# A decoder step on one core: reciprocal roots on ScalarE, the first factors on another queue, a longer warm-up, and a new order of squares, pooling steps and low parts

## The chip, the core and the metric

The kernel runs on one NeuronCore of a Trainium2 chip. TensorE multiplies matrices into PSUM, VectorE, ScalarE and GpSimd work on rows of 128 partitions, and SyncE (SP) issues most DMAs. The metric is device time in microseconds (us) of one execution.

## The reference

One step of a decoder layer over 288 rows: 256 new positions of one sequence and 8 x 4 new positions of running sequences.

```
h = rmsnorm(x, norm1_g)
a, gate, z = split(h @ w_in + b_in)                 # 2048 -> 3 x 1024
u = a * sigmoid(gate)
c = silu(layernorm(depthwise_conv31(history + u)))  # 1024 channels
d = window_sum(z) / count - z                       # windows 2, 4, 8, 16
p = (d @ pool_w per group) * pool_scale
x = x + concat(c, p) @ w_out                        # 2048 -> 2048
f = square(relu(rmsnorm(x, norm2_g) @ w_ff1))       # 2048 -> 8192
y = rmsnorm(x + f @ w_ff2, norm_f)
```

It also returns the last 30 rows of u and the last 15 of z. Everything is float32.

## The kernel before

Channels lie on the partitions, the 288 rows along the free dimension. Each float32 operand is split into a high part, the value rounded to TensorE's fp32r format, and a low part, the rest. A product of 128 x 128 weights with 128 x 288 values is then three matmuls: high by high, low by high, high by low. That makes 8112 matmuls of 288 columns, and TensorE's order of them is the kernel's spine.

*Weights.* `load` brings a block of 1024 x 256 in two DMAs of 512 KB into a ring of six raw tiles, and `split_part` makes both parts of each, into a ring of five pairs. ScalarE always casts the high part (L274). The low part comes in one of three ways, by a letter in the table `WAYS` (L73): V, VectorE subtracts (L279); G, GpSimd subtracts in two halves (L282); D, ScalarE writes the negated high part (L276) and GpSimd issues a DMA that adds the raw weights from memory to it (L277). A key such as `c3` names a stage, with one letter for each of its four parts; the fallback is the key's first letter. The feed-forward stage, `ff`, is all V.

*Stages.* Input projection in the order `c0 c1 c2 c3 c4 p3 c5 p2 P3 c6 p1 P2 p0 P1 c7 P0`: a `c` is a pair of 128 conv channels and their gates, a `p` one pooling group of 256 channels, a `P` that group's small product with pool_w. Each `c` and `p` has 96 matmuls, each `P` 12. Then w_out over the pooling half (eight groups of 48 matmuls), w_out over the conv half, and four chunks of w_ff1 and w_ff2.

*The first stage.* c0 and c1 run together, over eight pairs of 128 input rows. For each pair `first_split` loads x and weights, casts the high weights (L364, L371), scales x by the norm's gain into `hx` (L367 on VectorE for the first, L369 on ScalarE), and forms the low parts (L373, L376). Nine float32 products of a constant run ahead, as a warm-up (L214). `squares` sums x squared for the first norm (ScalarE L418, VectorE L420 to L422), held back by a small copy that reads the third pair's high weights (L413); `rsqrt_sums` turns the sums into reciprocal roots (Sqrt on ScalarE, then reciprocal and a correction step on VectorE, L249 to L256), and `spread` copies them to all partitions by a product with the identity matrix. The row that results multiplies the projections later (L445, L483).

*Convolution.* VectorE does 30 of the 31 taps of each channel block (L461) at low priority: the block stands in `later()`, which adds to the scheduler's priority number. A smaller number goes first.

*Order.* A scheduler with a planned timeline lays each engine's instructions out ahead of the run, by priority among those that are ready in its plan. `tc.issue_after(x)` puts an instruction behind x on its engine. In the middle of the kernel `mm` chains every matmul behind the last one (up to the product P1); `between` hands a function to `gemm` that puts a norm's small products ahead of a given k of a group.

*The end.* The last product's rows are summed, `inverse_root` (L231 to L236) forms the factors, and `finish` (L715 to L721) scales and stores in pieces, in turn on SP's and ScalarE's DMA queues.

Of the kernel before, what the change touches and what calls it, by code (L numbers as in the profile page):

```python
# [72 lines left out]
WAYS = {"c2": "GVGV", "c3": "GDGG", "c4": "GDGD", "p3": "GDDG", "c5": "GDGD", "c": "GGGV", "p": "GVVG", "w0": "VV", "w": "GG", "ff": "VV"}  # L73
# [13 lines left out]
def trunk_kernel(ctx: ExitStack, tc: tile.TileContext, io):  # L87
# [110 lines left out]
    nc.sync.dma_start(vec[:, 0:NG], io["vec"][:, 0:NG])  # L198
# [8 lines left out]
    def load_table(func, src):  # L207

        return nc.scalar.activation(few[: src.shape[0], :], src, func)

    load_table(AF.Sqrt, ones[:, 0:1])
    warm = ms("warm")
    for j in range(9):
        nc.tensor.matmul(warm[:, 0, 0:P], ones, ones, start=True, stop=True)  # L214
# [16 lines left out]
    def inverse_root(mean, root, y, out):  # L231

        nc.vector.reciprocal(y, root)
        nc.vector.scalar_tensor_tensor(out=root, in0=mean, scalar=EPS, in1=y, op0=ALU.add, op1=ALU.mult)
        nc.vector.scalar_tensor_tensor(out=root, in0=root, scalar=-0.5, in1=y, op0=ALU.mult, op1=ALU.mult)
        nc.vector.scalar_tensor_tensor(out=out, in0=root, scalar=1.5, in1=y, op0=ALU.add, op1=ALU.mult)  # L236

    def rsqrt_sums(parts, scale, after=None):

        pq = ms("pt")
        pt = pq[:, 0, :]
        for n, t in enumerate(parts):
            for j in range(3):
                last = mm(pt[:TB, j : j + 1], t[:, j * TB : (j + 1) * TB], ones[:, 0:1], start=n + j == 0, stop=n == len(parts) - 1 and j == 2)
        st = const.tile([TB, 12], F32, name=nm("st"))
        s = [st[:, 3 * j : 3 * j + 3] for j in range(4)]
        nc.vector.tensor_scalar(s[0], pt[:TB, 0:3], scale * DC, EPS, op0=ALU.mult, op1=ALU.add)  # L249
        nc.scalar.activation(s[1], s[0], AF.Sqrt)  # L250
        if after is not None:
            load_table(after, s[1][:, 0:1])
        nc.vector.reciprocal(s[2], s[1])
        nc.vector.tensor_tensor(s[3], s[2], s[2], op=ALU.mult)
        nc.vector.scalar_tensor_tensor(out=s[3], in0=s[3], scalar=-0.5, in1=s[0], op0=ALU.mult, op1=ALU.mult)
        nc.vector.scalar_tensor_tensor(out=s[2], in0=s[3], scalar=1.5, in1=s[2], op0=ALU.add, op1=ALU.mult)  # L256
        return s[2], pq[:, 1, :T], last
# [99 lines left out]
    hx, firsts = [], []  # L357

    def first_split(k0):
# [5 lines left out]
        for k in range(k0, k0 + 2):  # L365
            if k == 0:
                nc.vector.tensor_scalar(hx[k][0], xT[:, k, :], v("norm1_g", k), None, op0=ALU.mult)  # L367
            else:
                nc.scalar.activation(hx[k][0], xT[:, k, :], AF.Copy, scale=v("norm1_g", k))  # L369
        for b in blocks[1:]:  # L370
            nc.scalar.copy(hi[:, b], raw[:, b])  # L371
        for b in blocks:
            nc.vector.tensor_tensor(lo[:, b], raw[:, b], f32(hi[:, b]), op=ALU.subtract)  # L373
# [37 lines left out]
    def squares():  # L411

        nc.scalar.copy(scratch[:, :, :, 0:1], f32(firsts[2][0])[:, 1, 1, 0:10].rearrange("p (n k t) -> p n k t", n=5, t=1))  # L413
        for q in range(8):
            xq = xT[:, 2 * q : 2 * q + 2, :]
            a = q // 4
            dst = scratch[:, 2 + q % 3] if q % 4 else tot[a]
            nc.scalar.activation(dst, xq, AF.Square)  # L418
            if q % 4:
                nc.vector.tensor_tensor(tot[a], tot[a], dst, op=ALU.add)  # L420
# [19 lines left out]
    def conv_pair(i, banks):  # L440
        up = u_all[:, i, 0:UO]
        us = samples(u_all[:, i, UO:UL], US)
        ta, gate = [b[:, :T] for b in banks]
        for b in (gate, ta):
            nc.vector.tensor_tensor(b, b, rb, op=ALU.mult)  # L445
        tg = tmpp.tile([P, 2, T], F32, name=nm("tg"), tag="ag", bufs=2)[:, 0, :]
        nc.scalar.activation(tg, gate, AF.Sigmoid, bias=v("b_in", 8 + i))
        for out, a, b in ((up[:, CH:UO], ta[:, :SEQ], tg[:, :SEQ]), (us[:, :, CH:US], samples(ta[:, SEQ:T], NS), samples(tg[:, SEQ:T], NS))):
            nc.vector.scalar_tensor_tensor(out=out, in0=a, scalar=v("b_in", i), in1=b, op0=ALU.add, op1=ALU.mult)
# [27 lines left out]
    def pool_group(g):  # L477
# [17 lines left out]
        first_sums = s[:, :, PH : PH + w - 1]  # L495
        nc.gpsimd.tensor_tensor(first_sums, first_sums, rcnt[:, None, w - 2 : 2 * w - 3].to_broadcast([P, 2, w - 1]), op=ALU.mult)
        nc.vector.scalar_tensor_tensor(out=d[:, :, 0:SEQ], in0=s[:, :, PH:ZO], scalar=1.0 / w, in1=z[:, :, PH:ZO], op0=ALU.mult, op1=ALU.subtract)
        news = [x[:, :, ZO:ZL].rearrange("p m (b t) -> p m b t", t=ZS)[:, :, :, PH:] for x in (s, z)]
        nc.gpsimd.tensor_scalar(news[0], news[0], 1.0 / w, None, op0=ALU.mult)
        nc.gpsimd.tensor_tensor(d[:, :, SEQ:T].rearrange("p m (b t) -> p m b t", t=NS), news[0], news[1], op=ALU.subtract)  # L500
        dh, dl = act2("dx", tag="p", bufs=4)
        nc.scalar.copy(dh, d)
        nc.vector.tensor_tensor(dl, d, f32(dh), op=ALU.subtract)
# [20 lines left out]
    def first_sums():  # L524
        diag.append(rsqrt_sums(squares(), 1.0 / D, AF.Sigmoid))
        return diag[0][2]

    def first_rows():
        pr, last = spread(diag[0])
        nc.scalar.copy(rb, pr)  # L530
        return last
# [16 lines left out]
    load_table(AF.Sqrt, f32(mixp[1][0])[:, 0:1])  # L548
# [12 lines left out]
    def ln_sums():  # L561
        ssc = None
        for c in cs:
            nc.vector.tensor_tensor(c, c, norm["mean"][:, None, :].to_broadcast([P, 2, T]), op=ALU.subtract)
            q = tmpp.tile([P, 2, T], F32, name=nm("q2"), tag="ag" if ssc is None else "ag2", bufs=2)
            nc.scalar.activation(q, c, AF.Square)
            if ssc is None:
                ssc = q
            else:
                nc.vector.tensor_tensor(ssc, ssc, q, op=ALU.add)  # L570
        nc.vector.tensor_tensor(ssc[:, 0, :], ssc[:, 0, :], ssc[:, 1, :], op=ALU.add)
        norm["sums"] = rsqrt_sums([ssc[:, 0, :]], 1.0 / DC, AF.Silu)
        return norm["sums"][2]

    def ln_rows():
        norm["rows"], last = spread(norm["sums"])
        return last

    BETWEEN = {5: {4: ln_mean}, 6: {6: ln_sums}, 7: {2: ln_rows}}
# [10 lines left out]
    for j, c in enumerate(cs):  # L590
        n = tmpp.tile([P, 2, T], F32, name=nm("n"), tag="ag", bufs=2)
        nc.vector.tensor_tensor(n, c, norm["rows"][:, None, :].to_broadcast([P, 2, T]), op=ALU.mult)  # L592
        for m in range(2):
            i = 2 * j + m
            nc.scalar.activation(n[:, m, :], n[:, m, :], AF.Silu, bias=v("ln_b", i), scale=v("ln_g", i))  # L595
        mh, ml = act2("mx")
        nc.scalar.copy(mh, n)  # L597
# [40 lines left out]
    def second_rows():  # L638
# [9 lines left out]
        nc.scalar.activation(root, mean, AF.Sqrt, bias=eps)  # L648
        inverse_root(mean, root, r2, r2)
# [57 lines left out]
    root, first, s_f = [cst[:TB, 2 + 3 * j : 5 + 3 * j] for j in range(3)]  # L707
    nc.scalar.activation(root, sums_f, AF.Sqrt, bias=eps[:TB, :])
    inverse_root(sums_f, root, first, s_f)
# [13 lines left out]
    finish(nc.vector, rows_f, ((0, 1), (1, 1), (2, 2), (4, 2), (6, 3), (9, 3)))  # L723
# [60 lines left out]
```

## Time and profile before

| | |
|---|---|
| three runs, us | 1084.15, 1084.95, 1085.42; median 1084.95 |
| the profiled execution, us | 1084.57, its span 1082.8 |
| busy in the span, us | TensorE 1071.5, VectorE 635.4, ScalarE 479.0, GpSimd 173.6 |
| GB/s read and written, mean over the span | 175 |

In the profile a row of the view by time has the start, the length in us, the engine (PE is TensorE, PEld its weight loads, DVE VectorE, ACT ScalarE, POOL GpSimd; a q behind the name is the engine's instruction queue, which issues DMAs), the line of the kernel, the operation, what it writes and reads, and how many it merges. What stands in brackets is the engine's idle time before it and what ended it. A row of the view by stretches has the stretch, its length, then busy us and count for PE, PEld, DVE, ACT and POOL, the granted TensorE clock, the DMA engines' share and GB/s; instructions that only touch a stretch's edge are counted. A row of the view by groups has the line, engine, operation, shapes and count, then the total busy us and the mean ns of one, and behind the second bar the idle time before them. The chain of waits gives the start, the length and what the time was spent on. Tile names: `whi`, `wlo` the parts of the weights, `hx` the scaled x, `dx` a pooling operand, `mx` a conv operand, `ac` and `pp` accumulators.

### The profile page before, as it was taken

What the parts mean: (1) busy time and instruction counts of PE and PEld (TensorE: products, weight loads), DVE (VectorE), ACT (ScalarE), POOL (GpSimd) and SP (SyncE); (2) the same over time, 40 slices, a digit from 0 to 9 for tenths busy, and PEclk for the clock granted to TensorE, in tenths of its full rate; (3) what the DMA queues carried; (4) which work ended last, traced back from release to release, by engine and by line L of the source; (5) the groups of instructions that cost most, each with busy time, mean ns of one, the idle gap of its engine ahead of it and who ended that gap; (6) DMA issues with size and microseconds to landing.
All of it is one profiled execution on the core that took longest, in us unless ns stands there. A gap on an engine that the chain in (4) does not pass through costs nothing.

```text
span 1082.8 us, 19572 instructions
## 1 busy us (share of the span) xinstructions
PE 1071.5 (99%) x8198; PEld 1069.9 (99%) x8198; DVE 635.4 (59%) x818; ACT 479.0 (44%) x585; POOL 173.6 (16%) x180
## 2 busy tenths in 40 slices
PE   9999999999999999999999999999999999999996
PEld 9999999999999999999999999999999999999996
DVE  8899999678655544445544444545544445554553
ACT  8654445475544433334443333444433334444441
POOL 0878979512000000000000000000000000000001
PEclk9999999999999999999999999999999999999998
DMA  9896468545555555555555555555555555555522
GB/s 325 281 273 185 137 196 239 176 152 177 173 164 170 172 166 169 174 164 169 171 168 168 175 165 169 174 167 167 174 165 168 174 169 165 173 166 168 173 78 88
DMA packets 58296, 190.71 MB, mean 176 GB/s; under 512 B 6240, under 2 KB 11232, under 8 KB 58208
## 3 DMA queue, kind: packets, MB, share of 16 engines
q1 hardware_dynamic: 56336, 184.35, 53.9%
q0 software_dynamic: 1008, 3.67, 1.9%
q8 instruction: 64, 1.05, 0.4%
q10 hardware_dynamic: 864, 1.44, 0.4%
q14 instruction: 24, 0.20, 0.1%
HBM read 185.16 MB, written 4.28 MB: 175 GB/s over the span
## 4 chain that ended last, share of the span: by engine, by line
PE 77%; issue 20%; ACT 1%; DVE 0%; DMA 0%; POOL 0%; POOLq 0%
PE ac L305 77%; PE pp L305 1%; DMA wr<-in_w 0%; ACT whi L274 0%; POOL xT L720 0%; ACT n L595 0%; DVE wlo L279 0%; PE pt L305 0%; PE pmean L305 0%; POOLq L770 0%; DVE xT L695 0%; DVE n L592 0%; ACT whi L364 0%; ACT mx L597 0%; DVE hx L367 0%
## 5 line engine op out<-in xcount | busy, mean ns | idle before, releaser
L274 ACT CAST whi<-wr 128x1024 fp32r<-128x1024 f32 (+1 forms) x332 | 348.0, 1049 | 551.4 <-PE ac L305 533.5
L279 DVE TENSOR_TENSOR wlo<-wr,whi 128x1024 fp32r<-128x1024 f32 x288 | 353.1, 1226 | 348.5 <-ACT whi L274 348.5
L305 PE MATMUL ac<-ax,whi 128*128 128x288 f32 x2048 | 351.0, 292 | 0.0
L305 PE MATMUL ac<-fx,whi 128*128 128x288 f32 x2048 | 350.2, 292 | 0.0
L305 PEld LDWEIGHTS ac<-ax,whi 128*128 128x128 f32 x2048 | 296.0, 187 | 0.0
L305 PEld LDWEIGHTS ac<-fx,whi 128*128 128x128 f32 x2048 | 295.6, 187 | 0.0
L305 PE MATMUL ac<-ax,wlo 128*128 128x288 f32 x1024 | 217.4, 292 | 0.0
L305 PE MATMUL ac<-fx,wlo 128*128 128x288 f32 x1024 | 216.4, 292 | 0.0
L305 PEld LDWEIGHTS ac<-ax,wlo 128*128 128x128 f32 x1024 | 162.6, 187 | 0.0
L305 PEld LDWEIGHTS ac<-fx,wlo 128*128 128x128 f32 x1024 | 162.3, 187 | 0.0
L305 PE MATMUL ac<-hx,whi 128*128 128x288 f32 x768 | 131.8, 295 | 1.2 <-DVE hx L367 1.2
L720 POOL TENSOR_TENSOR xT<-xT,rf 128x288 f32<-128x288 f32 x4 | 3.1, 795 | 800.1 <-ACT rf L724 800.1
L305 PEld LDWEIGHTS ac<-hx,whi 128*128 128x128 f32 x768 | 112.1, 190 | 1.4 <-ACT hx L369 1.4
L282 POOL TENSOR_TENSOR wlo<-wr,whi 128x512 fp32r<-128x512 f32 x74 | 100.3, 1410 | 35.3 <-ACT whi L274 34.3
L461 DVE SCALAR_TENSOR_TENSOR pc<-u_all,vec,pc 128x256 f32<-128x256 f32 x232 | 99.5, 483 | 1.9 <-ACT pc L458 0.7
L305 PE MATMUL ac<-hx,wlo 128*128 128x288 f32 x384 | 80.1, 294 | 0.0
L305 PEld LDWEIGHTS ac<-hx,wlo 128*128 128x128 f32 x384 | 61.1, 190 | 0.0
L305 PE MATMUL ac<-dx,whi 128*128 128x288 f32 x256 | 46.0, 296 | 0.0
L305 PE MATMUL ac<-mx,whi 128*128 128x288 f32 x256 | 45.1, 294 | 0.1
L664 DVE SCALAR_TENSOR_TENSOR t<-ac,r 128x576 f32<-128x576 f32 x32 | 24.2, 758 | 25.1 <-PE ac L305 25.1
L305 PEld LDWEIGHTS ac<-dx,whi 128*128 128x128 f32 x256 | 38.0, 188 | 0.2
L305 PEld LDWEIGHTS ac<-mx,whi 128*128 128x128 f32 x256 | 37.5, 188 | 0.6 <-ACT mx L597 0.4
(133 smaller groups left out, 533.6 us busy)
## 6 DMA issues: line engine op xcount, KB each, us to landing
wr<-in_w SPq DMA_DIRECT2D x335, 512.0 KB, 3.8
wlo<-in_w POOLq DMA_DIRECT2D x7, 512.0 KB, 7.7
xT<-in_xT SPq DMA_DIRECT2D x8, 288.0 KB, 7.3
wr<-in_w SPq DMA_DIRECT2D x5, 256.0 KB, 3.6
out_u_out<-u_all SPq DMA_DIRECT2D x1, 1208.0 KB, 9.3
u_all<-in_hist_c SPq DMA_DIRECT2D x8, 136.0 KB, 6.2
out_z_out<-z_all SPq DMA_DIRECT2D x1, 668.0 KB, 9.9
z_all<-in_hist_p SPq DMA_DIRECT2D x4, 152.0 KB, 7.5
```

The lines of the kernel that those rows point to most:

```text
L274: nc.scalar.copy(hi, raw)
L279: nc.vector.tensor_tensor(lo, raw, f32(hi), op=ALU.subtract)
L282: nc.gpsimd.tensor_tensor(lo[:, j : j + 2, :], raw[:, j : j + 2, :], f32(hi[:, j : j + 2, :]), op=ALU.subtract)
L305: last = nc.tensor.matmul(*args, **kw)
L461: nc.vector.scalar_tensor_tensor(out=dst, in0=up[:, w : w + SEQ], scalar=cwv[:, w : w + 1], in1=pc, op0=ALU.mult, op1=ALU.add)
L664: nc.vector.scalar_tensor_tensor(out=t, in0=bk[:, :, :T], scalar=0.0, in1=both(rows2[0]), op0=ALU.max, op1=ALU.mult)
L720: eng.tensor_tensor(xk, xk, r[:, None, :].to_broadcast([P, n, T]), op=ALU.mult)
```

## The change

- The first norm's gains (`vec`, 16 columns) are loaded by GpSimd's DMA queue, not SP's.
- Reciprocal roots: ScalarE's Abs_reciprocal_sqrt replaces Sqrt and VectorE's reciprocal, in the two norms by columns, the second norm and the last one; the mean is read from PSUM and eps comes in as the activation's bias. Table loads ask for the new function.
- Eleven warm-up products for nine.
- In the first stage, the low weights of the first pair are issued behind `hx` of the first rows on VectorE; the holding copy goes, and the square of pair q is issued behind the scaling of pair q + 2.
- High priority (`later(-LATER)`) for: the first sums and rows; evaluating the first two conv pairs; the last steps of pooling groups 1 and 0; the layer norm's sums and rows.
- The layer norm's rows are asked for ahead of k = 0 of w_out's last pooling group, for k = 2; the activations of a conv pair are issued behind the cast of the pair before it.
- `WAYS`: one D becomes V in c3 and in c4, one V becomes G in p0 and in c7.
- One output piece of two rows becomes two of one.

```diff
-WAYS = {"c2": "GVGV", "c3": "GDGG", "c4": "GDGD", "p3": "GDDG", "c5": "GDGD", "c": "GGGV", "p": "GVVG", "w0": "VV", "w": "GG", "ff": "VV"}
+WAYS = {"c2": "GVGV", "c3": "GVGG", "c4": "GVGD", "p3": "GDDG", "c5": "GDGD", "c7": "GGGG", "c": "GGGV", "p0": "GVGG", "p": "GVVG", "w0": "VV", "w": "GG", "ff": "VV"}
...
-    nc.sync.dma_start(vec[:, 0:NG], io["vec"][:, 0:NG])
+    nc.gpsimd.dma_start(vec[:, 0:NG], io["vec"][:, 0:NG])
...
-    load_table(AF.Sqrt, ones[:, 0:1])
+    load_table(AF.Abs_reciprocal_sqrt, ones[:, 0:1])
     warm = ms("warm")
-    for j in range(9):
+    for j in range(11):
...
-    def inverse_root(mean, root, y, out):
-        nc.vector.reciprocal(y, root)
-        nc.vector.scalar_tensor_tensor(out=root, in0=mean, scalar=EPS, in1=y, op0=ALU.add, op1=ALU.mult)
-        nc.vector.scalar_tensor_tensor(out=root, in0=root, scalar=-0.5, in1=y, op0=ALU.mult, op1=ALU.mult)
-        nc.vector.scalar_tensor_tensor(out=out, in0=root, scalar=1.5, in1=y, op0=ALU.add, op1=ALU.mult)
+    def inverse_root(mean, y, t, out, after=None):
+        nc.scalar.activation(y, mean, AF.Abs_reciprocal_sqrt, bias=eps[: y.shape[0], :])
+        if after is not None:
+            load_table(after, y[:, 0:1])
+        nc.vector.scalar_tensor_tensor(out=t, in0=mean, scalar=EPS, in1=y, op0=ALU.add, op1=ALU.mult)
+        nc.vector.scalar_tensor_tensor(out=t, in0=t, scalar=-0.5, in1=y, op0=ALU.mult, op1=ALU.mult)
+        nc.vector.scalar_tensor_tensor(out=out, in0=t, scalar=1.5, in1=y, op0=ALU.add, op1=ALU.mult)
-    def rsqrt_sums(parts, scale, after=None):
+    def rsqrt_sums(parts, column, after=None):
...
-        nc.vector.tensor_scalar(s[0], pt[:TB, 0:3], scale * DC, EPS, op0=ALU.mult, op1=ALU.add)
-        nc.scalar.activation(s[1], s[0], AF.Sqrt)
...
+        inverse_root(mean, st[:, 0:3], t, st[:, 4:7], after=after)
+        return st[:, 4:7], pq[:, 1, :T], last
...
+        scaled_x.append(last.ins)
         for b in blocks[1:]:
             nc.scalar.copy(hi[:, b], raw[:, b])
         for b in blocks:
-            nc.vector.tensor_tensor(lo[:, b], raw[:, b], f32(hi[:, b]), op=ALU.subtract)
+            with tc.issue_after(first.ins) if k0 == 0 else nullcontext():
+                nc.vector.tensor_tensor(lo[:, b], raw[:, b], f32(hi[:, b]), op=ALU.subtract)
...
-        nc.scalar.copy(scratch[:, :, :, 0:1], f32(firsts[2][0])[:, 1, 1, 0:10].rearrange("p (n k t) -> p n k t", n=5, t=1))
...
-            nc.scalar.activation(dst, xq, AF.Square)
+            with tc.issue_after(scaled_x[min(q + 2, 7)]):
+                nc.scalar.activation(dst, xq, AF.Square)
...
+        with later(-LATER if i < 2 else 0):
             ta, gate = [b[:, :T] for b in banks]
...
+        with later(-LATER if g < 2 else 0):
             first_sums = s[:, :, PH : PH + w - 1]
...
     def first_sums():
-        diag.append(rsqrt_sums(squares(), 1.0 / D, AF.Sigmoid))
+        with later(-LATER):
+            diag.append(rsqrt_sums(squares(), mean_d, AF.Sigmoid))
...
-    BETWEEN = {5: {4: ln_mean}, 6: {6: ln_sums}, 7: {2: ln_rows}}
+    BETWEEN = {5: {4: ln_mean}, 6: {6: ln_sums}, 7: {0: ln_rows}}
...
-            nc.scalar.activation(n[:, m, :], n[:, m, :], AF.Silu, bias=v("ln_b", i), scale=v("ln_g", i))
+            with tc.issue_after(copied) if j else nullcontext():
+                nc.scalar.activation(n[:, m, :], n[:, m, :], AF.Silu, bias=v("ln_b", i), scale=v("ln_g", i))
         mh, ml = act2("mx")
-        nc.scalar.copy(mh, n)
+        copied = nc.scalar.copy(mh, n).ins
...
-    finish(nc.vector, rows_f, ((0, 1), (1, 1), (2, 2), (4, 2), (6, 3), (9, 3)))
+    finish(nc.vector, rows_f, ((0, 1), (1, 1), (2, 1), (3, 1), (4, 2), (6, 3), (9, 3)))
```

More of the change, by code (lines that the diff above doesn't have):

```diff
@@ L547, in trunk_kernel @@
             pool_products(i)
-    load_table(AF.Sqrt, f32(mixp[1][0])[:, 0:1])
+    load_table(AF.Abs_reciprocal_sqrt, f32(mixp[1][0])[:, 0:1])
     with later(2 * LATER):
@@ L706, in trunk_kernel @@
                 nc.tensor.matmul(idle[:, 0:P], ones, ones, start=True, stop=True)
-    root, first, s_f = [cst[:TB, 2 + 3 * j : 5 + 3 * j] for j in range(3)]
-    nc.scalar.activation(root, sums_f, AF.Sqrt, bias=eps[:TB, :])
-    inverse_root(sums_f, root, first, s_f)
+    s_f = cst[:TB, 6:9]
+    inverse_root(sums_f, cst[:TB, 2:5], ends[:TB, 0, 4:7], s_f)
     for spread_f in (rows_f, again):
```

88 lines of the change are left out of this document (41 added, 47 removed).

## The prediction

> **What bounds the kernel now.** I read the page's busy times first, then the busy time by stretches, then the first 30 us and the last 13 us in order of time.
>
> ```profile
> PE 1071.5 (99%) x8198; PEld 1069.9 (99%) x8198; DVE 635.4 (59%) x818; ACT 479.0 (44%) x585; POOL 173.6 (16%) x180
> ```
>
> TensorE is busy for all but 11 us of 1082.8. The number of its matmuls is not changed by the diff (two more warm-up products aside), so only time in which it runs slowly or stands still can go. The stretches, with busy us and count for each engine, say where that is:
>
> ```profile
> 0.00:25.00 25.00, 22.81 (x145) 22.55 (x146) 19.83 (x33) 20.37 (x37) 1.73 (x33) 1.00 0.92 330
> 6.40:10.37 3.97, 3.97 (x16) 3.97 (x17) 3.20 (x7) 3.13 (x7) 0.00 (x0) 1.00 1.05 408
> 10.50:14.47 3.97, 3.97 (x32) 3.97 (x31) 3.49 (x7) 3.93 (x8) 0.00 (x0) 1.00 1.05 409
> 105.00:180.00 75.00, 75.00 (x574) 74.90 (x574) 73.69 (x147) 39.73 (x60) 64.58 (x57) 1.00 0.63 184
> 219.00:220.95 1.95, 1.83 (x12) 1.33 (x11) 1.62 (x4) 1.95 (x3) 0.00 (x0) 1.00 0.34 107
> 285.00:290.00 5.00, 5.00 (x40) 5.00 (x39) 4.37 (x6) 2.35 (x4) 0.00 (x0) 1.00 0.38 116
> 300.00:350.00 50.00, 50.00 (x387) 50.00 (x386) 25.73 (x25) 21.91 (x24) 0.00 (x0) 1.00 0.54 170
> ```
>
> The steady pace is 50 / 387 = 0.13 us a matmul. From 6.40 to 10.37, "busy" throughout, only 16 ran, and 32 (with both edges) in an equal stretch right after: half pace, although the column of the granted clock says 1.00 for both. That costs 3.97 - 16 x 0.13 = 1.9 us, the largest loss in the trace. The row of 219.00 is a second place; from 285 on nothing is lost. In 105 to 180 VectorE has 73.7 of 75 us in use while TensorE never waits, so VectorE's order there is a risk, not yet a bound.
>
> **The change part by part.** The sum is made against the profiled execution, 1084.57 us (span 1082.8), which is 0.38 below the median of the runs shown, 1084.95.
>
> *The start.* First the rows of the first six microseconds and the landing of the factors:
>
> ```profile
> 0.73 0.39 SPq L198 DMA_DIRECT2D vec<-in_vec  x1
> 1.04 4.21 PE L214 MATMUL warm<-ones 128*128 128x128 f32 x18 [1.04 <-DVE cst L229]
> 1.18 0.41 SPq L191 DMA_DIRECT2D xT<-in_xT  x1
> 4.63 0.62 ACT L364 CAST whi<-wr 128x512 fp32r<-128x512 f32 x1 [1.97 <-DMA wr<-in_w]
> 5.28 0.69 DVE L373 TENSOR_TENSOR wlo<-wr,whi 128x512 fp32r<-128x512 f32 x1 [2.88 <-ACT whi L364]
> 5.59 0.54 ACT L369 ACTIVATE hx<-xT,vec 128x288 fp32r<-128x288 f32 x1 [0.35 <-DMA xT<-in_xT]
> 5.89 0.36 DVE L367 TENSOR_SCALAR hx<-xT,vec 128x288 fp32r<-128x288 f32 x1
> 6.40 1.30 PE L305 MATMUL ac<-hx,whi 128*128 128x288 f32 x4 [1.15 <-DVE hx L367]
> 12.67 0.20 ACT L413 COPY z_all<-whi 128x10 f32<-128x10 f32 x1
> 12.89 2.41 ACT L418 ACTIVATE z_all<-xT 128x576 f32<-128x576 f32 x4
> 15.21 1.04 ACT L364 CAST whi<-wr 128x1024 fp32r<-128x1024 f32 x1
> ```
>
> ```profile
> vec<-in_vec SPq DMA_DIRECT2D x1, 8.0 KB, 3.1
> ```
>
> The first real matmul waits for VectorE's hx at 6.25. That stood behind VectorE's low part (5.28 to 5.97) and behind xT, which landed just before 5.59. The change issues hx ahead of the low part, and takes the factors off SP's queue, so xT is issued 0.45 earlier (1.18 to 0.73). By both, hx on VectorE could end near 5.6; the second matmul needs ScalarE's hx, which follows a cast ending at 5.25 and took 0.54, so 5.8 at best. But two more warm-up products are four more records of 4.21 / 18 = 0.23, and the block ends at 1.04 + 22 x 0.234 = 6.2 instead of 5.25; a matmul can follow some 0.2 or 0.3 before the modelled end of the last. I take 6.1: -0.3 (ends 0 and -0.5). The factors' own landing on GpSimd's queue isn't in the trace. SP's took 3.1 from the issue, the accumulating transfers that GpSimd issues 5.8 to 9.8 (row below, but 512 KB each). The small one is nearer to 8 KB: with about 0.9 for GpSimd's issue, 0.7 + 0.9 + 3.1 = 4.7, ahead of xT. GpSimd's memsets stand behind it for those 0.9; nothing in the first stage's products reads them.
>
> *The half pace.* The block of 4.21 us did not end it, an idle 1.15 us followed, and then 4.0 us of real work did. With the longer block the idle time shrinks from 1.15 to near zero, so work is unbroken from 1.04 on. Ends: 0, if only work behind the real start counts, and -1.9, if all 16 run at full pace. Unbroken work of 4.21 was not enough once, 5.1 ahead of the real start may or may not be; I take the change of pace one microsecond after it: four slow matmuls left, 4 x 0.12 lost, -1.4.
>
> The Trainium skill (TensorE: Matmul & The Clock Gate, Part 1) says that the array starts at half rate and is released by a busy activity window of about 3.4 us that runs free of the kernel. The rows of the two paces agree; that the window runs free, one trace can't show. By the rule the release would lie, as an estimate, anywhere from 4.5 to 7.9 us, and the sum would be some 0.5 lower or 0.4 higher than mine.
>
> A faster TensorE reaches its inputs sooner. At 0.13 from 6.1 the fourth pair of rows is due at 6.1 + 72 x 0.13 = 15.5; ScalarE's cast for it began at 15.21 and ended at 16.25, 0.7 late, because four squares (2.41) and a copy (0.20) stood ahead of it. The diff drops the copy and holds square q behind the scaling of pair q + 2: one square instead of four, so the cast comes 1.8 earlier. No stall is left there.
>
> *Low parts.* Costs by kind:
>
> ```profile
> L279 DVE TENSOR_TENSOR wlo<-wr,whi 128x1024 fp32r<-128x1024 f32 x284 | 349.8, 1232 | 348.5 <-ACT whi L274 348.5
> L282 POOL TENSOR_TENSOR wlo<-wr,whi 128x512 fp32r<-128x512 f32 x74 | 100.3, 1410 | 35.3 <-ACT whi L274 34.3 <-issue 0.9
> L276 ACT ACTIVATE wlo<-whi 128x1024 fp32r<-128x1024 f32 x7 | 7.4, 1061 | 0.2
> ```
>
> c3 and c4 give VectorE 2 x 1.23, take 2 x 1.06 from ScalarE and two 512 KB transfers from GpSimd's queue; p0 and c7 take 2 x 1.23 from VectorE and give GpSimd 2 x 2 x 1.41. VectorE's total stays. None of it is on TensorE's path: 0. GpSimd's 5.6 fall into 105 to 180, where it is idle for 75 - 64.6 = 10.4. What stays tight is the transfer kind in p3:
>
> ```profile
> DMA to landing us min/median/max: 5.8/7.7/9.8
> ```
>
> ```profile
> 66.07 0.88 POOL L277 DMA_DIRECT2D wlo<-in_w  x1
> 75.87 0.42 PE L305 MATMUL ac<-hx,wlo 128*128 128x288 f32 x2
> ```
>
> Issued at 66.07, at the slowest 9.8 it lands at 75.87, just when the low part is multiplied. Its issue follows a buffer that TensorE frees, so it moves with TensorE; two transfers fewer before it help. I take 0, with up to +1.7 as the other end (the gain of the start).
>
> *Pooling at high priority.* The first product of group 1 had this order (chain of waits, then VectorE in order of time):
>
> ```profile
> 138.27 21.71 PE ac L305 x167
> ...
> 159.98 0.53 PE pp L305 x4
> ```
>
> ```profile
> 158.52 0.75 DVE L503 TENSOR_TENSOR dx<-d,dx 128x576 fp32r<-128x576 f32 x1
> ```
>
> Its low half was ready at 159.27 and it ran half a microsecond later, so TensorE did not wait. VectorE in this full stretch won't move with TensorE by itself, and half a microsecond is less than the start's gain; the priority puts the pooling steps ahead of convolution taps, and the taps become late instead, which are needed only for the layer norm's mean in the sixth group of w_out. The second product's scaled result delayed matmuls a little:
>
> ```profile
> 170.84 0.97 PE L305 MATMUL ac<-dx,whi 128*128 128x288 f32 x5
> 171.64 0.42 PE L305 MATMUL ac<-dx,wlo 128*128 128x288 f32 x2
> ```
>
> Five took 0.80 where 0.65 is normal: -0.1 (ends 0 and -0.15).
>
> *Layer norm.* The handover to the second half of w_out:
>
> ```profile
> 217.79 1.15 ACT L595 ACTIVATE n<-n,vec 128x288 f32<-128x288 f32 x2
> 218.84 1.23 ACT L597 CAST mx<-n 128x576 fp32r<-128x576 f32 x2
> 219.00 0.43 PE L305 MATMUL ac<-dx,whi 128*128 128x288 f32 x2
> 219.55 0.54 PE L305 MATMUL ac<-mx,whi 128*128 128x288 f32 x2
> ```
>
> TensorE waited for the first mx, and from 219.00 to 220.95 some ten matmuls began where 15 fit: 0.65. ScalarE did the second pair's activations (1.15) ahead of the first mx; the change holds them behind it, and asks for the rows 12 matmuls earlier (k = 0 for k = 2, 1.6). The first mx then comes at least 1.15 sooner, more than the wait. What is late next is the low half on VectorE: I take -0.5 (ends 0 and -0.65). The roots on ScalarE drop a reciprocal in each place; at 285 TensorE had 5.00 of 5.00, so 0 there. Table loads keep their number and their cover.
>
> *The end.*
>
> ```profile
> 1071.57 0.17 DVE L233 RECIPROCAL cst<-cst 96x3 f32<-96x3 f32 x1 [1.53 <-ACT cst L708]
> 1071.85 0.16 DVE L234 SCALAR_TENSOR_TENSOR cst<-ends,cst 96x3 f32<-96x3 f32 x1
> 1073.39 4.08 DVE L720 TENSOR_TENSOR xT<-xT,ends 128x288 f32<-128x288 f32 x6 [1.00 <-PE ends L712]
> 1074.24 4.28 ACTq L721 DMA_DIRECT2D out_yT<-xT  x5
> ```
>
> This chain is bare: the reciprocal's step goes, 1071.85 - 1071.57 = -0.28. Cutting one output piece in two sends its first half earlier, adds one issue (4.28 / 5 at most 0.86, on SP) and shifts the last of VectorE's from ScalarE's queue to SP's: -0.15 (ends +0.2 and -0.3).
>
> Sum: 0.3 + 1.4 + 0.1 + 0.5 + 0.28 + 0.15 = 2.73; 1084.57 - 2.73 = 1081.8.
>
> **The rivals.** *The pace stays half for 4 us behind the real start.* For it: a block of 4.21 failed. Against it: the idle 1.15 behind it goes. Time: 1084.57 - (2.73 - 1.4) = 1083.2.
>
> *The inputs don't follow.* VectorE at 73.7 of 75 and p3's transfers keep their own time, and TensorE gives back the start's 1.7 at p3 or at group 1's product: 1083.5. For it the two margins above; against it, fewer transfers and the priority.
>
> *Factors late.* On GpSimd's queue they land as late as its usual transfer, 0.7 + 7.7 = 8.4: hx at 8.8, first matmul 2.5 later than before, half pace as before: 1083.2 + 0.3 + 2.5 = 1086.0. The Trainium skill (DMA: Bandwidth & Descriptors, Issuing engines are not separate DMA queues) speaks for part of it: another issuer saves only issue time; and its table gives GpSimd's path about 1 us to the first byte against 0.6. No run here shows a small transfer on it.
>
> *Slower: the product is asked for too early.* The matmuls' order is fixed ahead of the run. Group 1's product stands ahead of c7 in the written order, and ran 167 - 96 = 71 matmuls into c7. If the priority moves it ahead of c7 and VectorE's low half still comes at 159.27, TensorE waits up to 71 x 0.13 = 9.2: 1091.0. Slower by 0.2% (over 1087.1) needs a wait of 5.3, or 41 matmuls. Against it: the priority moves that same low half.
>
> **How the numbers follow.** The forecast's own range is 1080.8 (all far ends: 0.5 + 1.9 + 0.15 + 0.65 + 0.28 + 0.3 = 3.8) to 1082.8, chance 0.62. Half pace stays, 0.15; inputs don't follow, 0.09; factors late, 0.05; too early, 0.09. A measurement tells about 0.2% from no change, 2.2 us: faster is below 1082.8, the forecast's case and a share of the next, 0.64; same is the second to fourth, 0.24; slower 0.12, the last and what part of factors late exceeds it. The range 1080.8 to 1084.6 holds the first three but for a rest, 0.84.
>
> **What would show it.** In the changed profile: xT's issue near 0.73 and the first real matmul near 6.1, with over 25 matmuls in the 4 us behind it; no square between the third pair's scaling and the fourth's cast but one; the first mx without a wait of TensorE; the end chain without a reciprocal, the first output 0.28 sooner behind the last product. Wrong would make it: any wait of TensorE over 0.5 us between 30 and 220, at a low part by transfer or a pooling product, or 16 slow matmuls again.

## The result, and the profile after

The changed kernel is slower. Its median is 1088.05 us over nine runs (1086.43 to 1089.50), beside 1085.12 (1084.15 to 1085.80) for the kernel before in the same comparison: ratio 1.0027, 95% interval 1.0019 to 1.0035. The prediction was 1081.8, with a range of 1080.8 to 1084.6. The profiled execution took 1087.01 us with a span of 1085.2, and so stands 1.04 below its median; the profiled execution of before took 1084.57.

Four points of the work serve as milestones: the sums of the first norm (`pt`), the layer norm's mean (`pmean`), the last square (`q`) and the first output. First the kernel before, in order of time (its first output, at 1073.39, stands in the prediction):

```profile
32.47 0.59 PE L305 MATMUL pt<-ones,z_all 128*96 128x1 f32 x6
...
201.15 0.65 PE L305 MATMUL pmean<-sum_c,ones 128*128 128x288 f32 x2
...
1070.07 0.45 ACT L689 ACTIVATE q<-xT 128x288 f32<-128x288 f32 x1 [5.22 <-DVE xT L683]
```

The same in the changed kernel:

```profile
31.38 0.59 PE L299 MATMUL pt<-cst,z_all 128*96 128x1 f32 x6
...
204.18 0.65 PE L299 MATMUL pmean<-sum_c,ones 128*128 128x288 f32 x2
...
1072.42 0.44 ACT L691 ACTIVATE q<-xT 128x288 f32<-128x288 f32 x1 [5.23 <-DVE xT L685]
...
1075.47 4.14 DVE L721 TENSOR_TENSOR xT<-xT,ends 128x288 f32<-128x288 f32 x7 [1.00 <-PE ends L713]
```

| stretch | before | after | change |
|---|---|---|---|
| up to the first norm's sums | 32.47 | 31.38 | -1.09 |
| from there to the layer norm's mean | 168.68 | 172.80 | +4.12 |
| from there to the last square | 868.92 | 868.24 | -0.68 |
| from there to the first output | 3.32 | 3.05 | -0.27 |
| from there to the span's end | 9.41 | 9.73 | +0.32 |

Three of five stretches became shorter and the last a little longer; one gives all of the gain back and more. The view by stretches shows where in it (columns as in the prediction). The kernel before:

```profile
160.00:180.00 20.00, 20.00 (x151) 19.90 (x151) 19.96 (x42) 12.54 (x17) 16.26 (x14) 1.00 0.87 240
200.00:225.00 25.00, 24.88 (x185) 24.17 (x184) 18.84 (x28) 16.31 (x24) 4.53 (x4) 1.00 0.52 158
```

The changed kernel:

```profile
7.17:11.14 3.97, 3.97 (x30) 3.92 (x31) 3.97 (x8) 3.97 (x10) 0.00 (x0) 1.00 1.05 408
160.00:180.00 20.00, 17.15 (x123) 16.00 (x121) 19.82 (x43) 11.82 (x16) 13.50 (x13) 1.00 0.96 245
200.00:225.00 25.00, 25.00 (x190) 24.79 (x189) 18.42 (x26) 17.51 (x25) 7.40 (x6) 1.00 0.53 170
```

Between 160 and 180 us TensorE ran 123 matmuls for 151: 28 x 0.13 = 3.6 us lost. Around the layer norm it ran five more (0.65 gained), and the first four microseconds hold 30 matmuls for the 16 of before. The waits of TensorE between 140 and 225 us (engine, tile and line, what it waited for, us in total, times, longest); the same view lists none for the kernel before:

```profile
PE ac L299 <- DVE u_all L446: 1.0, 1, 1.0
PE pp L299 <- DVE dx L501: 0.8, 1, 0.8
PE ac L299 <- DVE wlo L273: 0.6, 1, 0.6
PE pp L299 <- DVE dx L513: 0.3, 1, 0.3
PE ac L299 <- ACT dx L512: 0.2, 1, 0.2
```

Four of five are for VectorE: the low half of pooling group 1 (`dx`, L501), a low part, the freeing of an accumulator by `u_all`, and the scaled product. The steps that lead to the first of them, in order of time:

```profile
151.70 5.50 POOL L276 TENSOR_TENSOR wlo<-wr,whi 128x512 fp32r<-128x512 f32 x4
154.51 1.53 DVE L495 SCALAR_TENSOR_TENSOR d<-s,z_all 128x512 f32<-128x512 f32 x1
158.01 0.84 POOL L497 TENSOR_SCALAR s<-s 128x64 f32<-128x64 f32 x1
160.01 0.68 ACT L500 CAST dx<-d 128x576 fp32r<-128x576 f32 x1 [2.59 <-POOL d L498]
161.26 1.21 DVE L273 TENSOR_TENSOR wlo<-wr,whi 128x1024 fp32r<-128x1024 f32 x1
161.49 0.42 PE L299 MATMUL pp<-dx,whi 128*128 128x288 f32 x2
163.18 0.75 DVE L501 TENSOR_TENSOR dx<-d,dx 128x576 fp32r<-128x576 f32 x1
163.98 0.81 PE L299 MATMUL pp<-dx,whi 128*128 128x288 f32 x4 [0.77 <-DVE dx L501]
```

The low half came at 163.18, where the kernel before had it at 158.52 (its row is in the prediction). GpSimd did four half low parts ahead of its own pooling step (158.01), and VectorE, once the cast was there, still did another low part first.

The start of the changed kernel, by time:

```profile
0.73 0.39 SPq L191 DMA_DIRECT2D xT<-in_xT  x1
1.04 4.92 PE L214 MATMUL warm<-ones 128*128 128x128 f32 x22 [1.04 <-DVE cst L229]
1.25 0.76 POOL L198 DMA_DIRECT2D vec<-in_vec  x1 [0.82 <-POOLq L767]
6.65 0.54 ACT L363 ACTIVATE hx<-xT,vec 128x288 fp32r<-128x288 f32 x1 [0.42 <-DMA vec<-in_vec]
6.65 0.37 DVE L361 TENSOR_SCALAR hx<-xT,vec 128x288 fp32r<-128x288 f32 x1 [5.41 <-DMA vec<-in_vec]
7.17 1.11 PE L299 MATMUL ac<-hx,whi 128*128 128x288 f32 x6 [1.21 <-DVE hx L361]
```

The 8 KB of factors took 5.4 us from the issue to the landing, where SP's queue took 3.1:

```profile
vec<-in_vec POOLq DMA_DIRECT2D x1, 8.0 KB, 5.4
```

So the first matmul came 0.77 later (7.17 for 6.40), and TensorE was still 1.09 earlier at the first norm's sums. The first weights came later too: ScalarE's cast of them ran from 5.62 to 6.24, where the kernel before had it at 4.63, so the first matmul could not have come before 6.24 even with the factors there.

### The profile page after: what moved, and what is told of

Same layout as the page of the kernel before. It is cut to its first block, busy times and chain, and to the rows that moved or that the text cites. A ratio compares the mean times of both kernels' runs of the same rounds, so it can differ in the third digit from the quotient of the medians.

```text
span 1085.2 us, 19576 instructions
## 1 busy us (share of the span) xinstructions
PE 1070.9 (99%) x8202; PEld 1068.8 (98%) x8202; DVE 633.4 (58%) x813; ACT 475.1 (44%) x582; POOL 177.1 (16%) x183
## 4 chain that ended last, share of the span: by engine, by line
PE 69%; issue 21%; DVE 5%; POOL 3%; DMA 1%; ACT 0%; POOLq 0%; ACTq 0%
PE ac L299 69%; DVE pc L458 2%; POOL s L489 1%; POOL wlo L276 1%; DMA wlo<-in_w 1%; DVE wlo L273 1%; DMA vec<-in_vec 0%; DVE d L495 0%; DVE dx L501 0%; POOL prd L461 0%; POOL xT L721 0%; PE pt L299 0%; ACT whi L268 0%; PE pp L299 0%; DVE dx L513 0%
## 5 line engine op out<-in xcount | busy, mean ns | idle before, releaser
L273 DVE TENSOR_TENSOR wlo<-wr,whi 128x1024 fp32r<-128x1024 f32 (+1 forms) x288 | 354.0, 1229 | 351.9 <-ACT whi L268 351.9
L276 POOL TENSOR_TENSOR wlo<-wr,whi 128x512 fp32r<-128x512 f32 x78 | 104.9, 1377 | 29.9 <-ACT whi L268 27.5
```

Of the source, the lines that this page charges most:

```text
L273: nc.vector.tensor_tensor(lo, raw, f32(hi), op=ALU.subtract)
L276: nc.gpsimd.tensor_tensor(lo[:, j : j + 2, :], raw[:, j : j + 2, :], f32(hi[:, j : j + 2, :]), op=ALU.subtract)
```

## The experiments

Two theories stood against each other. One: the new `WAYS` table puts more work ahead of the last pooling steps on VectorE and GpSimd, and TensorE waits for them. The other: the waits are the price of a TensorE that is early, whatever the table says. A third, smaller one was the later start.

| run | edit | median us | ratio to before, interval | matmuls 160 to 180 |
|---|---|---|---|---|
| the kernel before | | 1085.12 | | 151 |
| the changed kernel | | 1088.05 | 1.0027 (1.0019 to 1.0035) | 123 |
| e1 | after, c7 and p0 undone | 1084.98 | 1.0002 (0.9993 to 1.0011) | 139 |
| e2 | after, factors by SP | 1086.62 | 1.0013 (1.0004 to 1.0022) | 123 |
| e3 | after, c3 and c4 undone | 1083.80 | 0.9992 (0.9983 to 1.0001) | 145 |
| e4 | after, old output pieces | 1088.27 | 1.0028 (1.0016 to 1.0039) | 106 |
| e5 | after, whole table undone | 1082.64 | 0.9986 (0.9978 to 0.9995) | 153 |
| e6 | before, new table alone | 1090.05 | 1.0055 (1.0043 to 1.0067) | 111 |
| e7 | after, the two later parts by DMA | 1088.89 | 1.0041 (1.0029 to 1.0053) | 112 |
| e8 | before, eleven warm-up products | 1084.68 | 1.0000 (0.9992 to 1.0009) | 151 |
| e9 | after, table and pieces undone | 1082.24 | 0.9981 (0.9972 to 0.9989) | 153 |
| e10 | e9 with factors by SP | 1084.34 | 0.9994 (0.9985 to 1.0003) | 152 |
| e11 | after, c7 alone undone | 1084.34 | 0.9999 (0.9990 to 1.0008) | 144 |
| e12 | after, p0 alone undone | 1086.22 | 1.0018 (1.0009 to 1.0027) | 125 |

The kernel before had medians of 1084.6 to 1084.9 beside the runs e1 to e12.

### The table, whole

e5 takes it out of the changed kernel, e6 puts it alone into the kernel before.

```diff
-WAYS = {... "c3": "GVGG", "c4": "GVGD", ... "c7": "GGGG", "c": "GGGV", "p0": "GVGG", "p": "GVVG", ...}
+WAYS = {... "c3": "GDGG", "c4": "GDGD", ... "c": "GGGV", "p": "GVVG", ...}
```

> The changed kernel with the whole WAYS table of before, all else changed. So far either pair of entries taken back gave 3 to 4 us (1085.0 and 1083.8 for 1088.1), so the two pairs do not add. Theory A (VectorE and GpSimd are full up to about 165 us, and each part more puts the last pooling steps off): with neither pair TensorE waits as little between 160 and 180 us as in the kernel before (0.1 to 0.6 us) and the time is 1082.5 to 1083. Theory B (TensorE, which is 1.1 us earlier at 31 us, outruns VectorE and GpSimd whatever the table says): about 1.1 us of waits come at 160 to 180 us, and the time is 1083.8 to 1084.5.

> The kernel before with the new WAYS table alone. Theory A (the table's parts put the pooling steps off, whether TensorE is early or not): TensorE waits 3 us or more between 160 and 180 us and the time is 1088 to 1089.5, more than in the changed kernel, as the gains of the other edits are missing. Theory B (the waits are the price of the earlier start): the time is 1085 to 1086.3.

e5: 1082.64, e6: 1090.05. The table alone costs 5.4 us either way (1088.05 - 1082.64; 1090.05 - 1084.6). The first of these differences is taken across two comparisons; with each run set beside the kernel before of its own comparison it is 4.9. Without the table every other edit together gains 2 us. The early TensorE is not what waits: in e6 it reached the first norm's sums later than in the changed kernel (31.84 for 31.38), and TensorE had the same five waits, of the same lengths, within 0.3 us of the same places. e6 has the old priorities as well, so the new ones are not needed for the waits either. VectorE and GpSimd, not TensorE, set the time at 163 us. The same steps in e5, by time:

```profile
150.72 1.35 DVE L495 SCALAR_TENSOR_TENSOR d<-s,z_all 128x512 f32<-128x512 f32 x1
152.16 0.38 POOL L497 TENSOR_SCALAR s<-s 128x64 f32<-128x64 f32 x1 [0.64 <-DVE d L495]
...
156.07 0.67 ACT L500 CAST dx<-d 128x576 fp32r<-128x576 f32 x1 [2.62 <-POOL d L498]
157.34 0.75 DVE L501 TENSOR_TENSOR dx<-d,dx 128x576 fp32r<-128x576 f32 x1
158.61 0.43 PE L299 MATMUL pp<-dx,whi 128*128 128x288 f32 x2
```

The low half is there 5.84 us sooner than in the changed kernel (157.34 for 163.18), and TensorE's first product follows it without a wait. What filled the difference is counted in the view by stretches, for one line of code at a time, from 32 us to the start of that low half (the stretch, its length, the engine's busy us and count, then the clock, the DMA share and GB/s). In e5, the taps of the convolution first, then VectorE's low parts, then GpSimd's half low parts:

```profile
32.00:157.34 125.34, 77.99 (x186) 1.00 0.72 213
32.00:157.34 125.34, 15.97 (x14) 1.00 0.72 213
32.00:157.34 125.34, 60.57 (x44) 1.00 0.72 213
```

In the changed kernel:

```profile
32.00:163.18 131.18, 81.04 (x195) 1.00 0.67 195
32.00:163.18 131.18, 18.27 (x14) 1.00 0.67 195
32.00:163.18 131.18, 65.20 (x48) 1.00 0.67 195
```

Nine more taps stand ahead on VectorE (3.05 us), and 2.30 us more of low parts. The taps are low-priority filler, which the plan put ahead. Of the low parts the count is the same, but the first of e5's 14 only touches the edge of the stretch, so that one more lies inside it, and those inside took longer, up to 2.08 us for 1.68. These two do not make the whole of it: over the two stretches VectorE is busy 125.29 us for 117.23, 8.06 more, and idle 5.89 for 8.11. Another 3.09 us lie in the steps `d` and `dx` of the pooling groups, which took longer (3.98 for 2.74 and 4.63 for 2.78); the last section returns to why.

GpSimd has four half low parts more ahead. In order of time, though, VectorE is late first: its step `d` starts 3.79 later than in e5 (154.51 for 150.72), ahead of GpSimd's own last steps. ScalarE's cast is then 3.94 later and the low half 5.84. In these two traces VectorE's queue accounts for nearly all of the delay, and GpSimd's extra half parts add little of their own between `d` and the cast. The plan did put the product back as well (its first matmul starts at 161.49 in the changed kernel and at 158.61 in e5, with no wait of TensorE before it in either), but by 2.9 us, not by 5.8.

### The table, by parts

e3 undoes c3 and c4, e1 undoes c7 and p0, e11 and e12 undo one of these two.

```diff
 # e3
-"c3": "GVGG", "c4": "GVGD"
+"c3": "GDGG", "c4": "GDGD"
 # e1: both lines; e11: the first; e12: the second
-"c7": "GGGG",
-"p0": "GVGG",
```

> The changed kernel without its two later edits of WAYS (the entries c7 and p0 go, so that one subtraction in the eighth convolution group and one in the first pooling group go back to VectorE). Theory A, these two put GpSimd's subtractions ahead of its last pooling steps: the about 4 us by which TensorE's waits between 160 and 180 us grew go away, the time falls from 1088.0 to about 1084.2, and in the trace the scaling of the new sums for pooling group 1 starts on GpSimd near 153 us again (158.0 in the changed kernel). Theory B, the two earlier edits (the third and fourth group's parts on VectorE) leave VectorE with a backlog that lasts to 160 us: the waits stay, 1087 to 1088. Theory C, the loss is the later start alone: 1088.

> The changed kernel without its two earlier edits of WAYS (c3 GDGG, c4 GDGD again, so that these two parts come as finished halves by DMA). Theory A (the two later parts, given to GpSimd, make the waits): they stay, 1088.0 within 0.5. Theory B (VectorE's backlog from the two earlier parts makes them): the waits at 160 to 180 us fall by 3 us or more, time about 1084.5. The 0.3 us that TensorE waits at 77 us for p3's half by DMA shows in either case whether more halves by DMA make that wait longer.

> The changed kernel with c7's fourth part back on VectorE; p0's third part stays on GpSimd. In the built order this moves the pooling products of group 1 ten places earlier in TensorE's queue and takes 7 of 9 taps from ahead of that group's low part on VectorE. If c7's part is what carries the cost of the later pair: 160 to 180 us has 1.5 to 2.5 us of TensorE's excess for 4.4 and the time is 1085 to 1085.5, as with both parts back. If p0's part carries it: 1087.5 to 1088.

> The changed kernel with p0's third part back on VectorE; c7's fourth part stays on GpSimd. In the built order only 3 of 9 taps go from ahead of pooling group 1's low part, and the pooling products keep their places. If c7's part carries the cost: the waits stay near 4 us and the time is 1087 to 1088. If p0's part carries it: 1085 to 1085.5. If the two share it: 1086 to 1087.

Undoing either pair gives most of the loss back, so no theory that blames one pair alone holds. Taken from the medians, e3 gains 4.25, e1 3.07, e11 3.71, e12 1.83, and all four parts together 5.4: the gains overlap. The start of pooling group 1's low half on VectorE adds up better: 157.34 in e5, 159.48 in e1 (only the early pair is on VectorE: +2.14), 159.52 in e3 (only the late pair is on GpSimd: +2.18), 163.18 with both. TensorE feels only what exceeds its slack, and with one pair the excess is small. Of the late pair c7 matters more: with its part back the half low parts that stand on GpSimd ahead of the pooling step are two fewer, and the first products of the group came at 159.16 with a wait of 0.4.

Beside e5, the early pair alone costs 2.3 us (e1) and the late pair alone 1.2 (e3). How much of each is the moved work itself, and how much the other order that the plan takes with it, these runs don't tell apart.

### The two later parts by DMA

```diff
-"c7": "GGGG", "p0": "GVGG"
+"c7": "GGGD", "p0": "GVDG"
```

> The changed kernel, with the two later parts (fourth part of c7, third of p0) as finished halves by DMA: neither VectorE nor GpSimd makes them, VectorE has the same work as in the changed kernel, GpSimd two subtractions less. Theory A1 (GpSimd's two subtractions ahead of its last pooling steps make the waits): TensorE waits no more than 1.5 us between 160 and 180 us, time about 1084.5. Theory A2 (VectorE's own work ahead of them makes the waits): 3 us and more of waits, 1087 to 1088. Rival: the halves come late, since the DMA share was 0.98 between 160 and 170 us, and TensorE waits for wlo from DMA for 1 us or more, time 1085.5 to 1087.

1088.89. The rival came true, and for more than it was priced at. In order of time:

```profile
163.98 0.85 PE L299 MATMUL ac<-hx,wlo 128*128 128x288 f32 x2 [4.11 <-DMA wlo<-in_w]
```

The transfer was that late, with the DMA engines' share at 0.96 in this stretch already in the changed kernel. GpSimd's two subtractions less did bring the cast for group 1 from 160.01 to 157.44, as A1 said, but with TensorE waiting elsewhere the time tells nothing between A1 and A2. The low half of group 1 tells more: with that cast 2.57 earlier it starts at 161.34, only 1.84 earlier, and still 4.00 later than in e5. Most of the delay is left with VectorE's own work ahead of it, as A2 said.

### The output's pieces

```diff
-finish(nc.vector, rows_f, ((0, 1), (1, 1), (2, 1), (3, 1), (4, 2), (6, 3), (9, 3)))
+finish(nc.vector, rows_f, ((0, 1), (1, 1), (2, 2), (4, 2), (6, 3), (9, 3)))
```

> The changed kernel with the output's first part in the six pieces of before (10 output transfers in all, not 11). From VectorE's first output product to the span's end it was 9.73 us in the changed kernel and 9.36 in the one before. If the extra piece makes that: 9.4 again, and 0.3 to 0.4 less time, about 1087.7. If the pieces cost nothing and the difference is one of transfers from run to run: 9.5 to 9.8, and a time within 0.2 of the changed kernel's.

> The changed kernel with the WAYS table and the six output pieces of before. In all traces so far the stretch from VectorE's first output product to the span's end is 9.69 to 9.74 us with seven pieces and 9.34 to 9.41 with six. If that is the pieces: 9.4 here and 0.3 less than with the table alone (1082.64), so 1082.3. If the end is spread over the runs: 1082.6.

e4's time, 1088.27, did not fall, although its end did: 9.34 us from the first output product to the span's end. e9 (the table undone too, so without the waits) was 1082.24 for e5's 1082.64, with an end of 9.38 for 9.69. Over all traces with six pieces the end takes 9.34 to 9.41, with one exception (e10, 9.68), and with seven 9.69 to 9.77. The extra piece costs 0.3 to 0.4 of this stretch. In the changed kernel the last large piece is the seventh and so goes to SP's queue; the transfers, with size and median us from issue to landing:

```profile
out_yT<-xT SPq DMA_DIRECT2D x1, 432.0 KB, 4.4
```

In the kernel before it was the sixth, on ScalarE's:

```profile
out_yT<-xT ACTq DMA_DIRECT2D x1, 432.0 KB, 3.6
```

With it SP's queue has nine of the sixteen blocks of rows and ScalarE's seven, for eight and eight. That this imbalance is the cause was not tried by itself.

e4's trace also shows how the waits vary, which can hide a gain of 0.3. Its program is that of the changed kernel up to the output, and yet the low half of group 1 came 1.58 later (164.76). By time:

```profile
151.18 5.04 POOL L276 TENSOR_TENSOR wlo<-wr,whi 128x512 fp32r<-128x512 f32 x4
154.00 3.62 DVE L495 SCALAR_TENSOR_TENSOR d<-s,z_all 128x512 f32<-128x512 f32 x1
...
156.16 0.91 POOL L489 TENSOR_TENSOR s<-z_all 128x422 f32<-128x422 f32 x1
...
165.56 1.21 PE L299 MATMUL pp<-dx,whi 128*128 128x288 f32 x4 [2.86 <-DVE dx L501]
```

VectorE's step `d`, 0.68 us where GpSimd is idle, took 3.62: it ended 0.55 after GpSimd's L489 (156.16 + 0.91 = 157.07, and 157.62). In the changed kernel's own trace the same step took 1.53, in e5 1.35.

### The factors' queue

```diff
-    nc.gpsimd.dma_start(vec[:, 0:NG], io["vec"][:, 0:NG])
+    nc.sync.dma_start(vec[:, 0:NG], io["vec"][:, 0:NG])
```

> The changed kernel with the first norm factors issued by SyncE again. If the factors' later landing (6.63 us for 3.87) is what delays the first matmul, it starts at about 6.4 us for 7.17 and the time falls by 0.8 to 1087.2. If the first weights (landed at 5.59 for 4.61 in the kernel before) are delayed by something else, the first matmul comes no earlier than 6.6 and the time falls by 0.3 at most. If an earlier start only lengthens the waits at 160 to 180 us, because VectorE and GpSimd set their end, the first matmul comes 0.8 earlier and the time stays at 1088.

> As the run beside it (table and pieces of before), with the first norm factors issued by SyncE again. If the later factors cost what the first matmul lost (7.17 for 6.40 us): the first matmul at 6.3 to 6.4 and 0.8 less, 1081.5. If an earlier start only meets weights that have not landed (in the kernel before with eleven warm-up products TensorE, at full pace, waited 0.66 us between 16 and 18 us): 0.1 to 0.3 less or the same, 1082.0 to 1082.4.

In e2 the first matmul came at 6.29, in e10 at 6.17, about 0.9 earlier. e2 is 1.4 us below the changed kernel's median, but the intervals touch (1.0004 to 1.0022 beside 1.0019 to 1.0035), its trace is no shorter (1087.33 for 1087.01), and the plan changed with it: that pair decides nothing. e10 beside e9 goes against both expectations: 1084.34 for 1082.24, 2.1 us slower with the earlier start. Seven of e9's eleven runs lie below all eleven of e10's, but these two intervals touch as well (0.9972 to 0.9989 beside 0.9985 to 1.0003), and here too the plan changed: the first product of the layer norm's mean starts at 201.73 for 196.85. By time, in e10:

```profile
7.46 0.62 ACT L366 CAST whi<-wr 128x512 fp32r<-128x512 f32 x1 [1.28 <-DMA wr<-in_w]
...
31.95 0.64 PE L299 MATMUL pt<-cst,z_all 128*96 128x1 f32 x6 [0.51 <-DVE z_all L418]
```

In e10 the second weights came late (cast at 7.46; at 7.09 in the changed kernel, where ScalarE, not the transfer, set it) and TensorE stood still 0.6 for that cast; the sums of squares came late too, and `pt` was at 31.95 for 31.38. Why they came late is not shown: the kernel before and e8 have the same order on SP's queue, and cast them at 6.79 and 6.80.

Of the 2.35 us between the two profiled executions (1084.51 and 1082.16) 0.57 are there at `pt`, 0.3 arise in a wait for a half by DMA at 50 us and 0.3 at the end. Another 0.9 is no wait at all. In the 36 us behind that wait TensorE ran a little slower, with the granted clock shown as 1.00. By stretches, e10 first and then e9:

```profile
51.00:87.00 36.00, 36.00 (x272) 36.00 (x271) 33.30 (x81) 20.99 (x26) 27.39 (x23) 1.00 0.95 255
51.00:87.00 36.00, 36.00 (x279) 36.00 (x278) 34.15 (x83) 21.43 (x28) 27.96 (x23) 1.00 0.96 260
```

Seven matmuls fewer are 7 x 0.13 = 0.9; the kernel before has 279 there too. Nothing shows that the edit causes this. So the factors on GpSimd's queue cost the first matmul 0.9, and the earlier start did not pay in e10; whether their queue decides the time stays open.

### The warm-up alone

```diff
-    for j in range(9):
+    for j in range(11):
```

> The kernel before with eleven warm-up products for nine and nothing else. If the longer warm-up makes TensorE's full pace from the first products: the half pace between 6.4 and 10.4 us goes (about 1.4 to 1.9 us). If that gain is carried to the end, the time is 1083.3 to 1083.7 for 1085.1; if VectorE and GpSimd set the time at 160 to 180 us, waits there take most of it back and the time is 1084.5 to 1085.1. If the half pace stays: 1085.1.

1084.68 for 1084.6: no difference, though the interval leaves room for 0.9 us either way. In its trace the first 3.97 us behind the first matmul hold 30 matmuls, so the pace was full. But e6, with nine warm-up products and the same start as the kernel before, has 30 as well, where the profiled execution of before has 16. The half pace is not in every execution, and so a count of warm-up products can't be judged by one trace. Part of where e8's full pace went is seen in the waits of the weight loads between 5 and 90 us:

```profile
PEld ac L305 <- DVE wlo L373: 0.5, 1, 0.5
PEld ac L305 <- ACT whi L364: 0.3, 1, 0.3
PEld ac L305 <- DMA wlo<-in_w: 0.2, 1, 0.2
```

The first two lie at 16 to 18 us, behind the four squares that the kernel before still does there (the changed kernel moved them and has no such wait), the third is p3's transfer. `pt` was 0.56 earlier (31.91), the last square 0.14.

## Why the prediction was wrong, by its steps

*Low parts: the step that failed.* "None of it is on TensorE's path: 0" was read from totals: VectorE's number of low parts does not change, and GpSimd has 10.4 us idle in 105 to 180. Both totals were right, and both were the wrong thing to sum. What counts is what stands ahead of the last pooling steps in two queues that run in order, and there VectorE had 8.06 us more to do before group 1's low half (3.05 of taps, 2.30 of low parts, 3.09 in pooling steps that took longer, less small change) and 2.22 us less idle time, and GpSimd four half low parts more. The low half came 5.84 us later than with the old table. The cover was half a microsecond, which the prediction had named. The step measured +5.4 us in the medians (e5, e6), 4.9 at the least, for 0.

*The rivals.* The forecast of the slower side had the right place, TensorE waiting for group 1's product, and the wrong cause and size: it blamed the priority for asking too early, at 9.2 us for one wait. The product was asked for later than before, the operand came later still, and five waits of 0.2 to 1.0 made 2.9 us together. The priority is not what makes them: e6 has them without it, and e5 has it without them. "The inputs don't follow" named the same product and VectorE's full queue, but priced them at what the start gains, 1.7, and not at what the table adds.

*"The priority puts the pooling steps ahead of convolution taps."* It put none ahead, with either table. From 32 us to group 1's low half 186 taps ran in the kernel before and 186 in e5, which adds the priority; with the new table 195 ran in e6 and 195 in the changed kernel. The count follows the table.

*The start.* -0.3 was +0.77. The failed term is the factors' landing: 4.7 by the estimate, 1.25 + 5.4 = 6.65 in the trace, where `hx` starts, since I took the small transfer for as fast as SP's behind the issue, 3.1, where it took 5.4 with its issue. The rival "factors late" had the mechanism at 8.4. It did not decide the time: with the earlier start e10 is 2.1 us slower and e2 1.4 faster.

*The half pace.* -1.4 by the longer warm-up. The pace was full, but e8 shows no gain for the warm-up and e6 full pace without it. Start and pace together were -1.09 at the first norm's sums, for -1.7.

*p3.* 0, up to +1.7: a wait of 0.3 of the weight loads in the changed kernel for this transfer, inside the bounds.

*Layer norm* -0.5: -0.68 in the stretch that holds it. *The reciprocal* -0.28: -0.27. *Output pieces* -0.15: +0.3 to +0.4; the term counted the issue and not the queue on which the last large piece then ends.

*The rest of the sum holds in total, by terms that miss both ways.* Without table and pieces the prediction's terms make 2.73 - 0.15 = 2.58 us; e9's profiled execution is 1084.57 - 1082.16 = 2.41 below that of before. The start and the pace gave 1.09 for 1.7, and the stretch from there to the last square 1.01 for 0.6. Some luck is in this: the 1.09 stands against an execution with the half pace, and e8 and e6, at full pace, reached `pt` 0.56 and 0.63 earlier with the old start. The medians agree with the total (1084.67 - 1082.24 = 2.43). That version, 1082.24 with a ratio of 0.9981 (0.9972 to 0.9989), is faster than both kernels.

## What to carry to other kernels

Sum the work on an engine that runs its queue in order up to the instruction that others wait for, not over the stretch: equal totals can hide more than five microseconds ahead of one step. Where an engine is 98% busy and the step after it has half a microsecond of slack, each edit that moves work between engines has to be priced at that step, and the low-priority filler counts as work. And an earlier first instruction is worth only what the inputs behind it allow: in e10 the first matmul came 0.9 earlier and the first norm's sums 0.57 later.

## What the runs showed of the hardware

*VectorE is held by GpSimd.* The step `d`, which reads two tensors in SBUF, takes 0.68 us with GpSimd idle and 1.35, 1.53 or 3.62 while GpSimd subtracts low parts; in each of these cases it ended about 0.55 us after one of GpSimd's instructions did. In e12 it took 0.68 beside a subtracting GpSimd too, so it is not held every time. The taps, which keep their sum in PSUM, were not held: in the changed kernel 17 of them took 6.74 us from 146.80, and 18 took 7.13 in e5, 0.40 each, with GpSimd busy throughout. Two executions of the same instructions differ by 2.1 us in it (e4 and the changed kernel), and the one that was held longer made TensorE wait 2.86 us. The Trainium skill (GPSIMD Engine Reference, Key points) states that GpSimd shares its SBUF interfaces with VectorE and contends with its instructions that have two inputs in SBUF; these rows agree, and add that the delay differs from run to run.

*Short waits can cost the clock.* e6 and the changed kernel have the same five waits. Behind them, in the stretch from 170 to 176 us, the changed kernel:

```profile
170.00:176.00 6.00, 4.67 (x34) 4.40 (x34) 6.00 (x16) 2.98 (x6) 6.00 (x5) 1.00 0.86 251
```

and e6:

```profile
170.00:176.00 6.00, 4.68 (x23) 4.21 (x22) 5.20 (x13) 1.98 (x4) 6.00 (x6) 0.72 0.89 279
```

As much busy time, 23 matmuls for 34, and a granted clock of 0.72 for 1.00: 11 x 0.13 = 1.4 us on top of the waits, in one execution and not in the other. e4 (after a wait of 2.86), e7 (after 4.11) and e2 (after waits of 1.73 and 0.35, 0.72 in the same stretch) show it too. The Trainium skill (TensorE: Matmul & The Clock Gate, Part 1) puts the return to half rate behind an idle window of about 3.4 us, and tells of another kernel in which short idle times were frequent enough for it; in e6 no single wait was longer than 1.04 us, so this trace goes with the second and not with the first. Both effects would make the changed kernel's times spread, as they do (3.07 us over nine runs, 1.65 for the kernel before), and would explain why its median lies 1.04 above its profile; no trace of that kernel shows it.
